# Scan mixer in a diffusion trunk: one exponential per head for both directions, convolution taps and gates in PSUM, heads in column halves

## The chip, the cores and the metric

The kernel runs on one core of a Trainium2 chip. The metric is the device time of one execution in microseconds (us); smaller is better. TensorE is written PE (its weight loads PEld), VectorE DVE, ScalarE ACT, GpSimd POOL, SyncE SP.

## What is computed

A trunk of four layers over 256 context tokens and 256 latent tokens of width 1024, in fp32. Layer 0 mixes tokens by differential attention, layer 1 by windowed attention, layer 2 by a scan in both directions, layer 3 again by differential attention; each mixer is followed by a gated FFN. The change is in layer 2's mixer, whose scan is this (32 heads in 4 groups, chunks of 128 tokens, both streams projected by one weight):

```python
xbc = silu(dwconv_centred(zxbcdt[...], conv_w, conv_b))       # 5 taps per channel
dt = softplus(zxbcdt[...] + dt_bias)                          # per direction and head
...
a_cs = cumsum(dt * A)                                         # within a chunk
seg = a_t[..., :, None] - a_t[..., None, :]
decay_in = exp(where(tril, seg, -inf))
cb = einsum('bclgn,bcsgn->bcgls', Cc, Bc)
y_diag = einsum('bcgls,bcghls,bcsghp->bclghp', cb, decay_in, xdt)
y_off = einsum('bclgn,bcghpn,bclgh->bclghp', Cc, prev, exp(a_cs))
...
y = (y_f + flip(y_b) + xs * d_skip) * silu(z)                 # then a norm and the output product
```

## The kernel before

All activations are kept feature-major, 128 features by 512 tokens (256 of context, 256 of latents). Weights come from HBM in fp32 by SP's queue; load_w (L255) splits each into a high and a low part, the high part by ACT (wh, L264), the low part by POOL (wl, L266), and lin (L283) makes each product of three matmuls, L291 to L293. All code is written straight-line; a scheduler sets each engine's order from the tiles' dependencies and the buffers that are free, and each engine then works through its list in that order. Names such as sc, sm, mm are tags: a tag has as many buffers as PSB or the tile's bufs say.

PSUM has eight banks: mm 2, ar 1, sc 2, sm 2, ad 1. In psum (L238) mm also takes the ar bank while no modulation rows are held, and the bank ad goes to the tag that EXTRA names for the mixer at work; for the scan mixer that is mm. So its products rotate over four banks, and sc has two.

ssd_mixer (L1287) goes through four groups of eight heads. A group has ten weight chunks: B, C, four of x, four of the gate z. chunk (L1304) is a product and conv_silu (L1076): ACT copies the product into a padded tile xpad (L1083), writes tap 0 with the bias into acc (L1089), DVE adds taps 1 to 4 one after another (L1097, in SBUF), ACT takes the tanh (L1100), DVE the last multiply (L1102). gate (L1310) halves the product by ACT (L1317), takes a tanh (L1318) and multiplies (L1319). In group 0 the two streams are projected one after the other, then ssd_dt (L1126) makes dt by a series on DVE (L1132 to L1146), the cumulative sums acs by small matmuls, and rows, the sums along the free dimension.

ssd_core (L1181) runs twice per group on four heads each. It transposes x to tokens, makes the chunk states (L1222 to L1236), and then for each head and each direction d: PE spreads a row of sums over all partitions (rb, L1247), POOL multiplies C·B by dt into cd (L1250), ACT makes four 128-wide steps Relu(acs - rb) into m (L1256), ACT takes exp(-m) (L1259), DVE multiplies m by cd (L1260). DVE then adds the two directions (L1262), and PE multiplies with the head's tokens into one half of the columns of yd (L1266), four matmuls of 128 columns. cd has two buffers (CDB), m three (DMB). After two heads DVE adds the skip term (L1271), and for each direction ACT takes er = exp(rb) (L1283), DVE multiplies it by the state product yo (L1284) and adds it to x (L1285). POOL also adds the squares for the group norm (L1340); finish (L1344) scales by it.

Of the kernel before, what the change touches and what calls it, by code (L numbers as in the profile page):

```python
# [180 lines left out]
class Trunk:  # L181
# [11 lines left out]
    EXTRA = ('sm', 'sc', 'mm')  # L193
    ENG_GATE = ENG_YO = 'vector'
    ENG_SSQ = 'gpsimd'
    ENG_CD = 'gpsimd'
    ENG_MADD = 'vector'
    ACTTAP = 0
# [157 lines left out]
    def ada_rows(self, i):  # L356
# [10 lines left out]
        self.acc = self.t([P, 6, 2, KD, 2], "acc")  # L367
# [261 lines left out]
    def ffn(self, i, u, streams, pool, gate, after, nxt):  # L629
# [53 lines left out]
        if nxt is not None:  # L683
            self.ada_rows(nxt)
# [391 lines left out]
    def conv_silu(self, ps, ci, dst, s, pool):  # L1076
# [9 lines left out]
        acc = self.t([P, 2, HALF], "cw", self.CW, pool=pool)[:, :ns]  # L1086
# [5 lines left out]
        if self.ACTTAP:  # L1092
            tm = self.t([P, 2, HALF], "cw", self.CW, pool=pool)[:, :ns]
            nc.scalar.activation(tm, xp[:, s0:s1, 4 : 4 + HALF], AF.Copy, scale=tap(4))
            nc.gpsimd.tensor_tensor(out=acc, in0=acc, in1=tm, op=AL.add)
        for j in range(1, 5 - self.ACTTAP):
# [29 lines left out]
    def ssd_dt(self, ps, pool):  # L1126
# [4 lines left out]
        v, e, q, p = w(), w(), w(), w()  # L1131
# [16 lines left out]
        self.dtt, at, self.acs, self.wst, self.dec = one("dtt"), one("at"), one("acs"), one("wst"), one("dec")  # L1148
# [15 lines left out]
        nc.scalar.activation(self.acs, acv, AF.Copy)  # L1164
        nc.scalar.activation(self.dec, totv, AF.Exp)
# [15 lines left out]
    def ssd_core(self, g, hf, bc, xf, sc, pool):  # L1181
# [58 lines left out]
        for j in range(2):  # L1240
            yd = self.psum("sc")
            for hh in (2 * j, 2 * j + 1):
                ms = []
                for d in range(2):
                    hd = 32 * d + h0 + hh
                    rb = self.psum("sc")
                    nc.tensor.matmul(rb, sel[d][:, hh, :], self.rows, start=True, stop=True)  # L1247
                    m = self.t([P, NT], "dm", self.DMB, pool=pool)
                    cd = self.t([P, NT], "cd", self.CDB, pool=pool)
                    getattr(nc, self.ENG_CD).tensor_tensor(  # L1250
                        out=cd.rearrange("p (c l) -> p c l", c=4), in0=cbm[d].rearrange("p (c l) -> p c l", c=4),
                        in1=self.dtt[:, :, hd : hd + 1].to_broadcast([P, 4, P]), op=AL.mult,
                    )
                    for c in range(4):
                        t = slice(c * P, (c + 1) * P)
                        nc.scalar.activation(  # L1256
                            m[:, t], rb[:, t], AF.Relu, scale=-1.0, bias=self.acs[:, c, hd : hd + 1]
                        )
                    nc.scalar.activation(m, m, AF.Exp, scale=-1.0)  # L1259
                    tt(out=m, in0=m, in1=cd, op=AL.mult)  # L1260
                    ms.append(m)
                getattr(nc, self.ENG_MADD).tensor_tensor(out=ms[0], in0=ms[0], in1=ms[1], op=AL.add)  # L1262
                r = 64 * (hh % 2)
                for c in range(4):
                    t = slice(c * P, (c + 1) * P)
                    nc.tensor.matmul(  # L1266
                        yd[r : r + 64, t], xtok[:, c, 64 * hh : 64 * hh + 64], ms[0][:, t], start=True, stop=True,
# [4 lines left out]
            for d in range(2):  # L1272
# [258 lines left out]
```

## Time and profile before

| | |
|---|---|
| median of three runs | 2726.39 us (2724.1 to 2736.12) |
| the profiled execution | 2728.86 us, its span 2726.7 us |
| PE busy | 2531.5 us (93%) |
| DVE busy | 1648.1 us (60%) |
| ACT busy | 1234.0 us (45%) |
| POOL busy | 1089.7 us (40%) |
| mean granted PE clock | 0.974 of full speed |

Shares are means over all stages. The scan mixer lies between about 1340 and 1890 us, its eight runs of ssd_core between 1425 and 1845. Busy time of an engine counts an instruction from its start to its end, waiting inside it included.

### The profile page before, as it was taken

The page shows a single profiled execution, that of the slowest core. Times are in us where ns is not written, and L with a number is a line of the kernel's source. Part 1 is how long each engine was busy: PE and PEld are TensorE (multiplying, and loading weights), DVE is VectorE, ACT ScalarE, POOL GpSimd, SP SyncE. Part 2 cuts the span into 40 slices and gives each one's busy share as a digit, 9 for nine tenths or more (in the row PEclk, how much of TensorE's full clock was granted, in tenths as well). Part 3 has the DMA queues.
Part 4 walks back from the last instruction along what each step waited for, and adds up shares of the span by engine and source line. Part 5 has one row for each costly group of instructions (what it writes and reads, how often), then busy time and mean ns, then how long its engine had stood idle before and what let it go on. Part 6 is the DMA issues. An engine that isn't in the chain of part 4 may idle for free.

```text
span 2726.7 us, 37430 instructions
## 1 busy us (share of the span) xinstructions
PE 2531.5 (93%) x13570; PEld 2089.7 (77%) x13570; DVE 1648.1 (60%) x3844; ACT 1234.0 (45%) x2514; POOL 1089.7 (40%) x525
## 2 busy tenths in 40 slices
PE   7899999999999999999988888889999998997998
PEld 4777688888776798888876666667988887876997
DVE  3776649931567649921689898866485116667112
ACT  5454553222557653222545565554432225555543
POOL 3322044444321054444243445442544443433784
PEclk9999999999999999999989899999999999999999
DMA  8333437742231147732221111123486323323452
GB/s 319 116 102 122 149 99 260 255 151 93 94 101 47 46 140 263 265 113 94 99 86 39 56 53 60 65 77 108 142 299 239 99 94 104 105 88 130 147 185 78
DMA packets 108040, 353.29 MB, mean 130 GB/s; under 512 B 14032, under 2 KB 24656, under 8 KB 105808
## 3 DMA queue, kind: packets, MB, share of 16 engines
q1 hardware_dynamic: 107280, 349.57, 38.1%
q8 instruction: 107, 1.75, 0.3%
q10 hardware_dynamic: 576, 1.34, 0.1%
q14 instruction: 77, 0.63, 0.1%
HBM read 329.36 MB, written 11.53 MB: 125 GB/s over the span
## 4 chain that ended last, share of the span: by engine, by line
PE 67%; DVE 14%; ACT 5%; issue 3%; DMA 2%; POOL 2%; DVEq 0%; ACTq 0%; SPq 0%; POOLq 0%
PE mm L291 6%; PE mm L292 6%; PE mm L293 6%; PE sc L291 5%; PE sc L293 5%; PE sc L292 5%; PE mm L302 4%; PE mm L303 4%; PE mm L301 4%; DVE dm L1260 2%; DVE cw L1097 2%; PE sc L303 1%; PE sc L301 1%; PE sc L302 1%; POOL wl L266 1%
## 5 line engine op out<-in xcount | busy, mean ns | idle before, releaser
L266 POOL TENSOR_TENSOR wl<-wr,wh 128x1024 fp32r<-128x1024 f32 x356 | 856.1, 2411 | 1354.9 <-ACT wh L264 1216.2
L264 ACT ACTIVATE wh<-wr 128x1024 fp32r<-128x1024 f32 x356 | 377.0, 1061 | 756.8 <-issue 277.1
L291 PE MATMUL mm<-uh,wh 128*128 128x512 f32 (+1 forms) x1136 | 406.5, 358 | 9.0 <-ACT uh L560 8.4
L293 PE MATMUL mm<-uh,wl 128*128 128x512 f32 (+1 forms) x1136 | 406.0, 357 | 0.0
L292 PE MATMUL mm<-ul,wh 128*128 128x512 f32 (+1 forms) x1136 | 405.4, 357 | 0.5 <-DVE sublng L861 0.4
L644 DVE TENSOR_TENSOR sc<-sc,sg 128x512 f32<-128x512 f32 (+1 forms) x100 | 57.5, 575 | 430.0 <-PE sc L293 423.2
L291 PE MATMUL sc<-uh,wh 128*128 128x512 f32 (+1 forms) x800 | 273.0, 341 | 0.7 <-DVE hid L647 0.7
L293 PE MATMUL sc<-uh,wl 128*128 128x512 f32 (+1 forms) x800 | 272.4, 341 | 0.0
L292 PE MATMUL sc<-ul,wh 128*128 128x512 f32 (+1 forms) x800 | 272.4, 340 | 0.0
L291 PEld LDWEIGHTS mm<-uh,wh 128*128 128x128 f32 x1136 | 219.6, 193 | 41.3 <-ACT uh L560 9.0
L292 PEld LDWEIGHTS mm<-ul,wh 128*128 128x128 f32 x1136 | 219.2, 193 | 30.2 <-issue 2.5
L293 PEld LDWEIGHTS mm<-uh,wl 128*128 128x128 f32 x1136 | 219.2, 193 | 27.8 <-issue 1.8
L303 PE MATMUL mm<-wl,hid 128*128 128x512 f32 x444 | 176.1, 397 | 0.0
L301 PE MATMUL mm<-wh,hid 128*128 128x512 f32 x444 | 176.1, 397 | 0.0
L302 PE MATMUL mm<-wh,hid 128*128 128x512 f32 x444 | 175.8, 396 | 0.0
L291 PEld LDWEIGHTS sc<-uh,wh 128*128 128x128 f32 x800 | 152.2, 190 | 17.7 <-DVE hid L647 0.9
L292 PEld LDWEIGHTS sc<-ul,wh 128*128 128x128 f32 x800 | 151.9, 190 | 16.8
L293 PEld LDWEIGHTS sc<-uh,wl 128*128 128x128 f32 x800 | 151.9, 190 | 16.9
L390 DVE SCALAR_TENSOR_TENSOR sq<-wa,sm 128x512 f32<-128x512 f32 x224 | 145.1, 677 | 0.1
L266 POOL TENSOR_TENSOR wl<-wa,wh 128x1024 fp32r<-128x1024 f32 x49 | 117.9, 2406 | 56.4 <-ACT wh L264 56.0
L1250 POOL TENSOR_TENSOR cd<-h,dtt 128x512 f32<-128x512 f32 x64 | 78.6, 1233 | 123.7 <-DVE dm L1260 117.6
L291 PE MATMUL ar<-uh,wh 128*128 128x256 f32 (+1 forms) x352 | 120.6, 343 | 0.0
(415 smaller groups left out, 5735.0 us busy)
## 6 DMA issues: line engine op xcount, KB each, us to landing
wr<-in_fin SPq DMA_DIRECT2D x154, 512.0 KB, 3.5
wa<-in_adat SPq DMA_DIRECT2D x144, 512.0 KB, 4.8
wr<-in_fout SPq DMA_DIRECT2D x77, 512.0 KB, 3.5
wr<-in_ssi SPq DMA_DIRECT2D x40, 512.0 KB, 3.5
wa<-in_adaw SPq DMA_DIRECT2D x36, 512.0 KB, 5.3
wr<-in_daqk SPq DMA_DIRECT2D x24, 512.0 KB, 3.7
wa<-in_fin SPq DMA_DIRECT2D x22, 512.0 KB, 3.5
wr<-in_sso SPq DMA_DIRECT2D x16, 512.0 KB, 3.5
```

The lines of the kernel that those rows point to most:

```text
L264: nc.scalar.activation(h, raw, AF.Copy)
L266: eng.tensor_tensor(out=l, in0=raw, in1=f32(h), op=AL.subtract)
L291: mm(out, wh, ah[ka][:, a:b], start=j == 0, stop=False)
L292: mm(out, wh, al[ka][:, a:b], start=False, stop=False)
L293: mm(out, wl, ah[ka][:, a:b], start=False, stop=j == len(todo) - 1)
L301: mm(out, ah[ka][:, tk], wt.h[:, kw, :], start=j == 0, stop=False)
L302: mm(out, al[ka][:, tk], wt.h[:, kw, :], start=False, stop=False)
L303: mm(out, ah[ka][:, tk], wt.l[:, kw, :], start=False, stop=j == len(todo) - 1)
L390: nc.vector.scalar_tensor_tensor(out=self.t([P, D], "sq", 2)[:, :512], in0=w[:, x, :], scalar=1.0, in1=self.arows[r, x], op0=AL.mult, op1= ...
L644: nc.vector.tensor_tensor(out=pu[:, :w], in0=pu[:, :w], in1=sg[:, :w], op=AL.mult)
L1097: nc.vector.scalar_tensor_tensor(out=acc, in0=xp[:, s0:s1, j : j + HALF], scalar=tap(j), in1=acc, op0=AL.mult, op1=AL.add)
L1250: getattr(nc, self.ENG_CD).tensor_tensor(out=cd.rearrange("p (c l) -> p c l", c=4), in0=cbm[d].rearrange("p (c l) -> p c l", c=4), in1=sel ...
```

## The change

In ssd_core the two directions of a head share one exponential. POOL multiplies C·B by dt for both directions (now L1245, into cd and m) and adds them (L1249): the two masked halves don't overlap but on the diagonal. PE spreads both rows into two PSUM banks. ACT writes rb[0] - acs into a tile f (L1257, four steps, with the negated sums nacs), DVE writes min(rb[1] - acs, f) into rb[1] (L1258, four steps), ACT takes one exponential in place in PSUM (L1262), DVE one multiply by cd (L1263). The tile f has one buffer, tag tf, which er uses too. The matmuls into yd come after both heads and alternate between the two column halves (L1269). er is no longer overwritten: DVE multiplies into yo in PSUM (L1287) and adds from there (L1288).

In conv_silu the sum of taps stays in the product's PSUM bank until the last multiply (L1087 to L1096); in gate the product is read from its bank and not halved, and the half goes into the multiply with y (L1335). ssd_dt runs after the latent stream's dt product, ahead of that stream's gates. EXTRA gives the bank ad to sc: three banks for sc, three for mm. The accumulators acc of the modulation's row sums come from the FFN's pool, and a pad tile is gone. Switches that were off (ACTTAP, ZB, ENG_GATE and others) are removed.

```diff
-    EXTRA = ('sm', 'sc', 'mm')
...
+    EXTRA = ('sm', 'sc', 'sc')
...
-        self.acc = self.t([P, 6, 2, KD, 2], "acc")
+        self.acc = self.t([P, 6, 2, KD, 2], "acc", pool=pool)
...
-        acc = self.t([P, 2, HALF], "cw", self.CW, pool=pool)[:, :ns]
+
+        acc = ps[:, : ns * HALF].rearrange("p (s t) -> p s t", s=ns)
...
         cbm = (sc["cbu"], sc["cbl"])
         for j in range(2):
-            yd = self.psum("sc")
+            ms = {}
             for hh in (2 * j, 2 * j + 1):
-                ms = []
+                hd = [32 * d + h0 + hh for d in range(2)]
+                m = ms[hh] = self.t([P, NT], "dm", self.DMB, pool=pool)
+                cd = self.t([P, NT], "cd", self.CDB, pool=pool)
+                eng = getattr(nc, self.ENG_CD)
+                for d, o in enumerate((cd, m)):
+                    eng.tensor_tensor(
+                        out=o.rearrange("p (c l) -> p c l", c=4), in0=cbm[d].rearrange("p (c l) -> p c l", c=4),
+                        in1=self.dtt[:, :, hd[d] : hd[d] + 1].to_broadcast([P, 4, P]), op=AL.mult,
+                    )
+                eng.tensor_tensor(out=cd, in0=cd, in1=m, op=AL.add)
+
+                rb = [self.psum("sc") for _ in range(2)]
                 for d in range(2):
...
-                    for c in range(4):
-                        t = slice(c * P, (c + 1) * P)
-                        nc.scalar.activation(
-                            m[:, t], rb[:, t], AF.Relu, scale=-1.0, bias=self.acs[:, c, hd : hd + 1]
-                        )
-                    nc.scalar.activation(m, m, AF.Exp, scale=-1.0)
-                    tt(out=m, in0=m, in1=cd, op=AL.mult)
-                    ms.append(m)
-                getattr(nc, self.ENG_MADD).tensor_tensor(out=ms[0], in0=ms[0], in1=ms[1], op=AL.add)
-                r = 64 * (hh % 2)
+                    nc.tensor.matmul(rb[d], sel[d][:, hh, :], self.rows, start=True, stop=True)
+                f = self.t([P, NT], "tf", 1, pool=pool)
                 for c in range(4):
                     t = slice(c * P, (c + 1) * P)
+                    nc.scalar.activation(f[:, t], rb[0][:, t], AF.Identity, bias=self.nacs[:, c, hd[0] : hd[0] + 1])
+                    stt(
+                        out=rb[1][:, t], in0=rb[1][:, t], scalar=self.acs[:, c, hd[1] : hd[1] + 1], in1=f[:, t],
+                        op0=AL.subtract, op1=AL.min,
+                    )
+                nc.scalar.activation(rb[1], rb[1], AF.Exp)
+                tt(out=m, in0=rb[1], in1=cd, op=AL.mult)
+            yd = self.psum("sc")
+            for c in range(4):
+                t = slice(c * P, (c + 1) * P)
+                for hh in (2 * j, 2 * j + 1):
+                    r = 64 * (hh % 2)
...
-                er = self.t([P, NT], "dm", self.DMB, pool=pool)
+                er = self.t([P, NT], "tf", 1, pool=pool)
...
-                    tt(out=er[:, t], in0=yo[:, t], in1=er[:, t], op=AL.mult)
-                    getattr(nc, self.ENG_YO).tensor_tensor(out=x[:, t], in0=x[:, t], in1=er[:, t], op=AL.add)
+                    tt(out=yo[:, t], in0=yo[:, t], in1=er[:, t], op=AL.mult)
+                    tt(out=x[:, t], in0=yo[:, t], in1=x[:, t], op=AL.add)
...
-            nc.scalar.activation(z[:, a:b], ps[:, :w], AF.Copy, scale=0.5)
             nc.scalar.activation(th[:, :w], ps[:, :w], AF.Tanh, scale=0.5)
             nc.vector.scalar_tensor_tensor(
-                out=z[:, a:b], in0=th[:, :w], scalar=1.0, in1=z[:, a:b], op0=AL.add, op1=AL.mult
+                out=z[:, a:b], in0=th[:, :w], scalar=1.0, in1=ps[:, :w], op0=AL.add, op1=AL.mult
             )
...
                     project_dt(wd, s)
+                    if s == "l":
+                        self.ssd_dt(pdt, pool)
                     for n in range(4):
                         gate(wz[n], zs[n], s)
                     for n in range(2):
                         chunk(ws[n], dst[n], ci[n], s)
-                self.ssd_dt(pdt, pool)
```

On DVE, in the middle of a run of ssd_core, before: dm is m, cd POOL's product, cw the convolution's sum and tanh, xpad its padded input, sm the state product.

```order
L1262 TENSOR_TENSOR dm_13675<-dm_13675,dm_13686 128x512
L1236 TENSOR_TENSOR h_12671<-sm_13668,h_12671 128x256
L1097 SCALAR_TENSOR_TENSOR cw_13912<-xpad_2552_12684,cwt_12672,cw_13912 128x512 x3
L1260 TENSOR_TENSOR dm_13702<-dm_13702,cd_13703 128x512
L1102 SCALAR_TENSOR_TENSOR bc_13837<-cw_13913,cw_13912 128x512
L1260 TENSOR_TENSOR dm_13713<-dm_13713,cd_13714 128x512
L1284 TENSOR_TENSOR dm_13734<-sm_13730,dm_13734 128x384
L1262 TENSOR_TENSOR dm_13702<-dm_13702,dm_13713 128x512
```

Now, in the same place: sc is the head's second bank of spread rows, tf the tile f, mm the bank that holds a chunk's sum of taps.

```order
L1258 SCALAR_TENSOR_TENSOR sc_13723<-sc_13723,acs_12986,tf_13726 128x128
L1335 SCALAR_TENSOR_TENSOR o_86<-o_86 128x512
L1258 SCALAR_TENSOR_TENSOR sc_13723<-sc_13723,acs_12986,tf_13726 128x128
L1091 SCALAR_TENSOR_TENSOR mm_13885<-xpad_2552_12686,cwt_12671,mm_13885 128x512
L1258 SCALAR_TENSOR_TENSOR sc_13723<-sc_13723,acs_12986,tf_13726 128x128
L1091 SCALAR_TENSOR_TENSOR mm_13925<-xpad_2551_12683,cwt_12671,mm_13925 128x512
L1258 SCALAR_TENSOR_TENSOR sc_13723<-sc_13723,acs_12986,tf_13726 128x128
L1096 SCALAR_TENSOR_TENSOR o_86<-cw_13911,mm_13885 128x512
L1091 SCALAR_TENSOR_TENSOR mm_13925<-xpad_2551_12683,cwt_12671,mm_13925 128x512 x2
L1263 TENSOR_TENSOR dm_13717<-sc_13723,cd_13718 128x512
```

A head's three operations on two SBUF tiles have become four narrow ones on PSUM, between which taps stand, and one multiply from PSUM.

On POOL, in the first run of ssd_core, before: h is the spilled C·B, dtt the dt, wl a weight's low part.

```order
L1250 TENSOR_TENSOR cd_13460<-h_12671,dtt_13179 128x512
L1250 TENSOR_TENSOR cd_13471<-h_12671,dtt_13179 128x512
L1250 TENSOR_TENSOR cd_13487<-h_12671,dtt_13179 128x512
L266 TENSOR_TENSOR wl_14379<-wr_14377,wh_14378 128x1024
L1250 TENSOR_TENSOR cd_13498<-h_12671,dtt_13179 128x512
```

Now, from the third head on:

```order
L1245 TENSOR_TENSOR dm_13436<-h_12670,dtt_12985 128x512
L1245 TENSOR_TENSOR cd_13437<-h_12670,dtt_12985 128x512
L1249 TENSOR_TENSOR cd_13437<-cd_13437,dm_13436 128x512
L263 TENSOR_TENSOR wl_14206<-wr_14204,wh_14205 128x1024
L1245 TENSOR_TENSOR cd_13457<-h_12670,dtt_12985 128x512
L1245 TENSOR_TENSOR dm_13456<-h_12670,dtt_12985 128x512
L1245 TENSOR_TENSOR dm_13644<-h_12670,dtt_12985 128x512
L1249 TENSOR_TENSOR cd_13457<-cd_13457,dm_13456 128x512
L263 TENSOR_TENSOR wl_14246<-wr_14244,wh_14245 128x1024
```

Each head has three operations where it had two, and a weight split stands behind an add that waits for both products.

On PE, the product of a head's m with its tokens, before: one head at a time, between matmuls of a chunk (ar) and transposes (sm).

```order
L293 MATMUL ar_13968<-uh_84,wl_13882 128x512
L291 MATMUL ar_13968<-uh_84,wh_13881 128x512
L292 MATMUL ar_13968<-ul_85,wh_13881 128x512
L1207 MATMUL sm_13622<-cst_base_67,o_86 128x128 x4
L293 MATMUL ar_13968<-uh_84,wl_13882 128x512
L1266 MATMUL sc_13456<-dm_13486,h_12671 64x128 x4
L291 MATMUL ar_13968<-uh_84,wh_13881 128x512
```

Now the two heads of a pair alternate; the pair's first matmul stands 18 rows further up.

```order
L289 MATMUL ar_13845<-ul_85,wh_13550 128x512
L290 MATMUL ar_13845<-uh_84,wl_13551 128x512
L1269 MATMUL ad_13476<-dm_13456,h_12670 64x128
L1269 MATMUL ad_13476<-dm_13436,h_12670 64x128
L1269 MATMUL ad_13476<-dm_13456,h_12670 64x128
L1269 MATMUL ad_13476<-dm_13436,h_12670 64x128
L1269 MATMUL ad_13476<-dm_13456,h_12670 64x128
L1269 MATMUL ad_13476<-dm_13436,h_12670 64x128
L1269 MATMUL ad_13476<-dm_13456,h_12670 64x128
L1253 MATMUL sc_13650<-rows_13037,sel_13608 128x512
```

Both heads' m must be there before the last seven; no matmul of the chunk stands between them any more.

## Rows read from the trace of the kernel before

**Rows 1.** The page: DVE's busy tenths in 40 slices, and the last chain.

```profile
DVE  3776649931567649921689898866485116667112
...
PE 67%; DVE 14%; ACT 5%; issue 3%; DMA 2%; POOL 2%; DVEq 0%; ACTq 0%; SPq 0%; POOLq 0%
```

**Rows 2.** By stretch: length; PE, PEld, DVE, ACT, POOL busy; clock; DMA share; GB/s.

```profile
500.00:600.00 100.00, 100.00 (x438) 81.99 (x437) 64.78 (x185) 25.64 (x30) 45.54 (x19) 1.00 0.62 201
800.00:900.00 100.00, 92.39 (x509) 64.19 (x507) 75.49 (x237) 73.42 (x214) 14.27 (x6) 1.00 0.16 47
1340.00:1390.00 50.00, 46.97 (x370) 45.73 (x371) 36.87 (x59) 29.31 (x61) 24.49 (x15) 1.00 0.44 141
1390.00:1425.00 35.00, 28.22 (x148) 22.82 (x147) 27.09 (x35) 12.03 (x20) 8.47 (x4) 0.80 0.16 53
1425.00:1845.00 420.00, 348.70 (x1611) 266.04 (x1610) 359.06 (x531) 232.35 (x546) 181.70 (x110) 0.93 0.18 60
```

**Rows 3.** Groups by line, 1425 to 1845: count; busy us, mean ns; idle before.

```profile
L1097 DVE SCALAR_TENSOR_TENSOR cw<-xpad,cwt,cw 128x512 f32<-128x512 f32 x82 | 81.2, 991 | 1.5 <-ACT cw L1089 0.6
L1250 POOL TENSOR_TENSOR cd<-h,dtt 128x512 f32<-128x512 f32 x64 | 78.6, 1233 | 123.7 <-DVE dm L1260 117.6 <-DVE h L1199 5.4 <-PE mm L292 0.7
L1260 DVE TENSOR_TENSOR dm<-dm,cd 128x512 f32<-128x512 f32 x64 | 70.4, 1103 | 33.2 <-ACT dm L1259 30.4 <-POOL cd L1250 2.7
L1262 DVE TENSOR_TENSOR dm<-dm,dm 128x512 f32<-128x512 f32 x32 | 39.9, 1246 | 0.1
L1222 DVE TENSOR_TENSOR v<-h,wst 128x256 f32<-128x256 f32 x48 | 28.3, 620 | 0.8 <-PE sm L1227 0.4 <-ACT h L1208 0.3
L1285 DVE TENSOR_TENSOR o<-o,dm 128x384 f32<-128x384 f32 (+2 forms) x47 | 24.3, 552 | 0.0
L1284 DVE TENSOR_TENSOR dm<-sm,dm 128x384 f32<-128x384 f32 (+2 forms) x47 | 19.5, 415 | 1.6 <-ACT dm L1283 1.6
L1232 DVE TENSOR_TENSOR h<-h,dec 128x256 f32<-128x256 f32 x32 | 18.0, 562 | 2.5 <-ACT h L1230 2.5
L1102 DVE SCALAR_TENSOR_TENSOR o<-cw,cw 128x512 f32<-128x512 f32 x15 | 13.1, 872 | 2.1 <-ACT cw L1100 2.1
```

**Rows 4.** Groups by line and shape, DVE, 1370 to 1900; columns as before.

```profile
L1284 DVE TENSOR_TENSOR dm<-sm,dm 128x384 f32<-128x384 f32 x16 | 8.8, 547 | 0.0
L1284 DVE TENSOR_TENSOR dm<-sm,dm 128x128 f32<-128x128 f32 x16 | 4.5, 284 | 1.6 <-ACT dm L1283 1.6
```

**Rows 5.** Single lines, whole span: count; duration ns least/median/most; first and last start; shapes.

```profile
L1260 DVE TENSOR_TENSOR dm<-dm,cd x64: 672/691/2872, 1428.5 to 1837.8; 128x512 f32<-128x512 f32 x64
L1271 DVE SCALAR_TENSOR_TENSOR o<-o,sng,sc x16: 734/746/748, 1449.0 to 1843.6; 128x512 f32<-128x512 f32 x16
L516 DVE SCALAR_TENSOR_TENSOR sc<-sc,rs_y,h x27: 742/749/752, 332.3 to 2721.7; 128x512 f32<-128x512 f32 x27
L1250 POOL TENSOR_TENSOR cd<-h,dtt x64: 1046/1112/2037, 1426.6 to 1828.6; 128x512 f32<-128x512 f32 x64
L1340 POOL TENSOR_TENSOR sq<-sq x12: 1267/1292/3026, 1479.6 to 1847.5; 128x512 f32<-128x512 f32 x12
```

**Rows 6.** Waits, 1425 to 1845: who <- for whom: us in total, times, longest.

```profile
POOL cd L1250 <- DVE dm L1260: 117.6, 47, 10.3
...
PE sc L1266 <- DVE dm L1262: 36.4, 26, 6.9
```

**Rows 7.** Instructions of PE in order of time: start us, us, line.

```profile
830.08 1.08 PE L1055 MATMUL sm<-swt,swv 128*64 128x256 f32 x8
...
1561.10 1.09 PE L1266 MATMUL sc<-dm,h 128*64 128x128 f32 x8 [0.27 <-DVE dm L1262]
```

**Rows 8.** Instructions of DVE in order of time: two chunks' first taps and last steps.

```profile
1570.21 3.90 DVE L1097 SCALAR_TENSOR_TENSOR cw<-xpad,cwt,cw 128x512 f32<-128x512 f32 x4
...
1576.24 0.68 DVE L1102 SCALAR_TENSOR_TENSOR bc<-cw,cw 128x512 f32<-128x512 f32 x1
...
1581.62 0.74 DVE L1097 SCALAR_TENSOR_TENSOR cw<-xpad,cwt,cw 128x512 f32<-128x512 f32 x1
...
1601.28 1.58 DVE L1102 SCALAR_TENSOR_TENSOR bc<-cw,cw 128x512 f32<-128x512 f32 x1
```

More of the change, by code (lines that the diff above doesn't have):

```diff
@@ L192 @@
     HEAD = 4
-    EXTRA = ('sm', 'sc', 'mm')
-    ENG_GATE = ENG_YO = 'vector'
+    EXTRA = ('sm', 'sc', 'sc')
     ENG_SSQ = 'gpsimd'
     ENG_CD = 'gpsimd'
-    ENG_MADD = 'vector'
-    ACTTAP = 0
     BC = 4
@@ L352, in ada_finish, with ada_rows @@
                 tt(out=mv, in0=pj, in1=gain, op=AL.mult)
-    def ada_rows(self, i):
+    def ada_rows(self, i, pool):
         nc = self.nc
@@ L683, in ffn @@
         if nxt is not None:
-            self.ada_rows(nxt)
+            self.ada_rows(nxt, pool)
         for p in range(0, n):
@@ L1091, in conv_silu @@
         )
[L1092 to L1096, printed above, removed]
+        for j in range(1, 5):
             nc.vector.scalar_tensor_tensor(
@@ L1130, in ssd_dt @@
         w = lambda: self.t([P, NT], "cw", self.CW, pool=pool)[:64]
-        v, e, q, p = w(), w(), w(), w()
+        v, e, p = w(), w(), w()
+        q = ps[:64]
         ts(out=v, in0=ps[:64], scalar1=self.dtp[:, 0:1], scalar2=None, op0=AL.add)
@@ L1147, in ssd_dt @@
         one = lambda n: self.t([P, 4, 64], n, pool=pool)
-        self.dtt, at, self.acs, self.wst, self.dec = one("dtt"), one("at"), one("acs"), one("wst"), one("dec")
+        self.dtt, self.acs, self.nacs, self.wst, self.dec = (one(n) for n in ("dtt", "acs", "nacs", "wst", "dec"))
+        at = self.t([P, HALF], "v", 4, pool=pool).rearrange("p (c h) -> p c h", c=4)
         for src, dst in ((v, self.dtt), (e, at)):
@@ L1164, in ssd_dt @@
         nc.scalar.activation(self.acs, acv, AF.Copy)
+        nc.scalar.activation(self.nacs, acv, AF.Copy, scale=-1.0)
         nc.scalar.activation(self.dec, totv, AF.Exp)
@@ L1240, in ssd_core @@
         for j in range(2):
-            yd = self.psum("sc")
+            ms = {}
             for hh in (2 * j, 2 * j + 1):
-                ms = []
-                for d in range(2):
[L1245 to L1252, printed above, removed]
-                    )
-                    for c in range(4):
-                        t = slice(c * P, (c + 1) * P)
-                        nc.scalar.activation(
-                            m[:, t], rb[:, t], AF.Relu, scale=-1.0, bias=self.acs[:, c, hd : hd + 1]
-                        )
-                    nc.scalar.activation(m, m, AF.Exp, scale=-1.0)
-                    tt(out=m, in0=m, in1=cd, op=AL.mult)
-                    ms.append(m)
-                getattr(nc, self.ENG_MADD).tensor_tensor(out=ms[0], in0=ms[0], in1=ms[1], op=AL.add)
-                r = 64 * (hh % 2)
@@ L1266, in ssd_core @@
+                nc.scalar.activation(rb[1], rb[1], AF.Exp)
[5 more added lines that the diff above has]
+                    r = 64 * (hh % 2)
                     nc.tensor.matmul(
-                        yd[r : r + 64, t], xtok[:, c, 64 * hh : 64 * hh + 64], ms[0][:, t], start=True, stop=True,
+                        yd[r : r + 64, t], xtok[:, c, 64 * hh : 64 * hh + 64], ms[hh][:, t], start=True, stop=True,
@@ L1331, in ssd_mixer @@
             zs = self.o[4 * ((g + 1) % 2) : 4 * ((g + 1) % 2) + 4]
-            for n in range(self.ZB):
-                zs[n] = self.t([P, NT], "zs", self.ZB, pool=pool)
             def gated(n):
-                getattr(nc, self.ENG_GATE).tensor_tensor(out=xg[n], in0=xg[n], in1=zs[n], op=AL.mult)
+                nc.vector.scalar_tensor_tensor(
+                    out=xg[n], in0=xg[n], scalar=0.5, in1=zs[n], op0=AL.mult, op1=AL.mult
+                )
                 d = 2 * (n > 0)
@@ L1479, in run @@
             self.prenorm(m[0], m[1], t)
-        self.t([P, 8], "pad")
         for n, (i, mix, ff) in enumerate(self.layers):
```

## The prediction, made before the changed kernel ran

> **What bounds the kernel now.** I read the slices first, then the busy table by stage, then the groups of the one stage that stands out, then single rows. Outside the scan mixer there is little to win: in the FFN the matmuls fill the engine, 100.00 of 100 us at clock 1.00 [rows 2]. In the slices DVE is at 9 tenths in one long block only, the scan mixer, and DVE holds 14% of the chain that ended last [rows 1]. By stage, from 1425 to 1845 us (the eight runs of ssd_core, 420 us) DVE is busy 359.06 us, PE 348.70 at a mean clock of 0.93, ACT 232.35, POOL 181.70 [rows 2]. DVE is the bound there: it idles 61 us, PE 71 us, and PE's largest waits are for L1262, the add that ends a head on DVE (36.4 us in 26 waits) [rows 6].
>
> What fills DVE is not arithmetic. L1260 multiplies two SBUF tiles: its fastest is 672 ns, its median 691, its longest 2872 [rows 5], its mean in this stage 1103 [rows 3]. The spread has the size of a POOL instruction: the two POOL forms here take 1112 and 1292 ns [rows 5]. The operations with one operand in PSUM show no spread: L1271 lies between 734 and 748 ns in 16 executions, L516, which reads and writes PSUM, between 742 and 752 in 27 [rows 5]. So DVE's operations on two SBUF tensors wait while POOL works, those with a PSUM operand do not.
>
> **The change part by part, core stage.** All sums are in DVE time of 1425 to 1845.
> The heads. Before, each of 32 heads costs two L1260 and one L1262: 70.4 + 39.9 = 110.3 us [rows 3]. After, it costs four 128-wide subtract-and-min operations and one 512-wide multiply, all with a PSUM operand. The multiply is 0.69 (the 691 of an undisturbed one). For the 128-wide one no row stands; L1284 goes from 547 ns at 384 columns to 284 at 128 [rows 4], 1.03 ns a column, so L516's 749 at 512 columns gives about 0.35 at 128. Sum: 32 x 0.69 + 128 x 0.35 = 66.9 us, **43.4 saved**. Undisturbed, the old form would cost 96 x 0.69 = 66.2 us: the arithmetic is no cheaper, all of the gain is waiting that disappears.
> The taps. 82 at 991 ns [rows 3] become PSUM in and out, 749 (L516's form): **19.8 saved**. The last step of the convolution: 15 at 872 [rows 3] become 0.69, **2.7 saved**; I don't count the rest of them and the gates.
> The off-diagonal add (L1285, 24.3) takes its other operand from PSUM and then costs what L1284 costs at the same sizes, 19.5 [rows 3]: **4.8 saved**.
> Against this, what stays on two SBUF tensors meets a busier POOL. L1222 and L1232 take 28.3 and 18.0 us [rows 3]; by an undisturbed 0.41 us for 256 columns (between L1284's 284 and 547) their 80 would take 32.8, so 13.5 us is waiting. POOL's share rises: 64 cd products at 1.112 and 32 new adds at 1.292 (L1340's form) make 112.5 where L1250 had 78.6, so 215.6 us of some 350 instead of 181.7 of 420, 62% for 43%. That scales 13.5 to 19.4: **6 lost**. DVE in sum: 43.4 + 19.8 + 2.7 + 4.8 - 6 = 64.7 us less.
>
> The other engines. ACT loses four of eight 128-wide steps and one of two exponentials per head, and has 188 us of idle time to begin with; it only gets lighter. PE: 348.70 busy at 0.93 would be 324 at full clock, less what the column halves give: eight matmul records of 256 columns on alternating halves take 1.08 us (L1055), eight of 128 columns, a head on one half, 1.09 (L1266) [rows 7], so alternating is twice as fast and up to 14 us of PE can go. At 420 - 65 = 355 us PE would be 87 to 91% busy, as in the attention mixer (92.39 of 100 [rows 2]): no bound yet, with little room left. I take nothing for it; that is the reserve under the larger gain below.
> POOL: at the start of a group a head waited for one cd product; now it waits for two products and an add. That is 1.112 + 1.292 = 2.4 us at three group starts, **7 lost** if nothing covers it; elsewhere its queue runs ahead, as today, where POOL waits 117.6 us for DVE to free cd [rows 6]. What queues behind a cd that waits is wl, the weight split that PE needs two chunks later.
>
> **Front of the mixer.** ssd_dt's chain moves from behind the two streams to ahead of the latent stream's gates. From 1390 to 1425 PE is busy 28.22 us at clock 0.80, 22.6 us' worth: 12.4 us are lost there, the bound of this gain; zero is the other. DVE has room, busy 64 of 85 us from 1340 [rows 2]. The chain then lies beside six half-width products: I take **10**, near the upper end, since nothing else holds PE there.
> The accumulators' new pool, the dropped pad, nacs (one copy) and the gate's halving moved into a multiply cost or give nothing I can price: all lie on DVE or ACT beside a full PE.
>
> Sum: -65 + 7 - 10 = -68 us. The profiled execution took 2728.86, 2.5 above the median; from it 2661, from the median of 2726.39 **2658 us**.
>
> [...]
>
> **The rivals.**
> 1. Half comes back as waiting. The products and the scan share more serial pieces: one tf tile serves all heads and both exponentials of the off-diagonal part, and a head's two selector banks are two of three. DVE's freed time then turns into idle time. For it: the engines run in a fixed order, and DVE already waits 61 us. Against: the two chains of four ACT steps per head become one. Half of 65, with the other terms: -33 + 7 - 10, **2690 us**.
> 2. More than forecast. If PE closes its idle time: 71 us of gaps and 348.70 x 0.07 = 24 us of slow clock, with 12 in front, -107: **2619 us**. It needs DVE to stop being late everywhere.
> 3. The change doesn't do what it says: operations with a PSUM operand wait for POOL as well when they also read SBUF, as the taps will. The heads then save nothing. +7 - 10: **2723 us**. Against: 43 undisturbed executions in two rows [rows 5].
> 4. Slower: the chunk's PSUM bank. Today four banks serve the products, each free after one copy; now there are three, held until the last step of the convolution. From first tap to last step is 1570.21 to 1576.92 in one chunk, 1581.62 to 1602.86 in another [rows 8]. With about 8 us of product and ACT before it a bank is held 15 to 29 us; six such and four gates of some 9 make 126 to 210 us per group on three banks, 42 to 70 us, under the 105 us that a group takes now. It decides from 46 us a chunk; at 50 a group takes 112 us, four of them 28 us more: **2754 us**. Against: the taps get shorter.
>
> **How the numbers follow.** Forecast 0.52, rival 1 0.21, rival 2 0.14, rival 3 0.07, rival 4 0.06. The range goes from rival 2 to a little beyond rival 1, 2618 to 2702, and leaves 3 and 4 out. About 0.5% (13.6 us) is what a measurement of this kernel tells from no change: forecast, 1 and 2 are faster by more (0.87), 3 is the same (0.07), 4 slower (0.06).
>
> **What would show it.** Right: the multiply at 0.69 us with hardly a spread, taps near 0.75, the small steps near 0.35; DVE some 295 us busy in a core stage of about 355; the clock there above 0.95; POOL near 216. Wrong: long waits of PE for a bank of mm or ar that DVE releases (rival 4); ACT waiting for the tf tile (rival 1); a multiply with a mean above 1 us (rival 3); DVE waiting for cd at many heads, which would make POOL's third operation dearer than 7 us.

## The result, and the profile after

| | before | after |
|---|---|---|
| median | 2725.24 us (2723.34 to 2736.12, 4 runs) | 2682.69 us (2681.79 to 2685.07, 4 runs) |
| ratio | 1 | 0.9837, 95% interval 0.981 to 0.9864 |
| profiled run / its span | 2728.86 / 2726.7 us | 2682.53 / 2680.7 us |

The change makes the kernel 44 us faster (37 to 52 by the interval); the forecast was 68. Its parts are best read in three places. First the single operations, over the whole span (count; duration ns least/median/most; first and last start; shapes). After the change L1263 is a head's multiply, L1258 its 128-wide step, L1091 a tap:

```profile
L1263 DVE TENSOR_TENSOR dm<-sc,cd x22: 676/691/693, 1420.5 to 1773.2; 128x512 f32<-128x512 f32 x22
L1258 DVE SCALAR_TENSOR_TENSOR sc<-sc,acs,tf x88: 345/354/364, 1415.6 to 1771.1; 128x128 f32<-128x128 f32 x88
L1091 DVE SCALAR_TENSOR_TENSOR mm<-xpad,cwt,mm x68: 476/748/757, 1360.4 to 1702.4; 128x512 f32<-128x512 f32 x60, 128x256 f32<-128x256 f32 x8
```

There is no spread left: the multiply's longest is 693 ns, where L1260's was 2872 [rows 5]. Second the groups of the core stage of after, 1415 to 1778 (count; busy us, mean ns; idle before), against [rows 3]:

```profile
L1091 DVE SCALAR_TENSOR_TENSOR mm<-xpad,cwt,mm 128x512 f32<-128x512 f32 x56 | 41.9, 748 | 1.3 <-ACT mm L1087 1.3
L1219 DVE TENSOR_TENSOR v<-h,wst 128x256 f32<-128x256 f32 x48 | 41.3, 911 | 2.2 <-ACT h L1205 1.9 <-PE sm L1224 0.3
...
L1258 DVE SCALAR_TENSOR_TENSOR sc<-sc,acs,tf 128x128 f32<-128x128 f32 x88 | 31.1, 354 | 2.6 <-ACT tf L1257 0.6
...
L1229 DVE TENSOR_TENSOR h<-h,dec 128x256 f32<-128x256 f32 x32 | 21.1, 660 | 2.1 <-ACT h L1227 2.1
L1091 DVE SCALAR_TENSOR_TENSOR ar<-xpad,cwt,ar 128x512 f32<-128x512 f32 x28 | 20.9, 747 | 0.0
...
L1263 DVE TENSOR_TENSOR dm<-sc,cd 128x512 f32<-128x512 f32 x22 | 15.1, 686 | 11.2 <-ACT sc L1262 10.4 <-POOL cd L1249 0.6
...
L1258 DVE SCALAR_TENSOR_TENSOR ad<-ad,acs,tf 128x128 f32<-128x128 f32 x40 | 14.1, 352 | 0.5
...
L1263 DVE TENSOR_TENSOR dm<-ad,cd 128x512 f32<-128x512 f32 x10 | 6.9, 686 | 2.7 <-ACT ad L1262 2.5
```

The heads cost 15.1 + 6.9 + 31.1 + 14.1 = 67.2 us of DVE, where they had cost 110.3. But L1219 (L1222 before) grew from 28.3 to 41.3.

Third the stretches (length; PE, PEld, DVE, ACT, POOL busy; clock; DMA share; GB/s). The whole mixer of before, up to a point 827 us ahead of the end (in the second half of the out-projection, whose last matmul starts 12 us later), and from its last off-diagonal add (1845.6) to that point:

```profile
1340.00:1900.00 560.00, 477.90 (x2378) 378.75 (x2379) 454.81 (x702) 297.62 (x676) 225.79 (x133) 0.94 0.22 72
1846.00:1900.00 54.00, 53.01 (x251) 43.33 (x250) 30.82 (x78) 23.40 (x50) 11.13 (x5) 1.00 0.32 111
```

The same of after: the mixer, its core, and from the last off-diagonal add (1777.4) to the same point of the program:

```profile
1340.00:1850.00 510.00, 458.74 (x2368) 362.32 (x2367) 390.57 (x766) 234.90 (x491) 253.32 (x164) 0.95 0.24 78
1415.00:1778.00 363.00, 326.96 (x1605) 247.98 (x1604) 300.53 (x600) 171.45 (x373) 204.99 (x140) 0.95 0.21 67
1778.00:1850.00 72.00, 66.33 (x305) 53.34 (x304) 38.19 (x77) 28.82 (x54) 21.06 (x9) 1.00 0.32 110
```

The last off-diagonal add comes 68 us earlier, the very number of the forecast. From there to the common point in the out-projection it is 54 us before and 72 after: 18 us are given back there, with PE busy 66 of 72 us at clock 1.00. The first output of the out-projection, which stands behind the last products of the mixer in PE's queue, comes at 1766.9 where it came at 1817.3 (lines under run 11): 50 us earlier, as much as the whole mixer gained.

```profile
L1408 ACT ACTIVATE o<-mm x5: 598/600/614, 1766.9 to 1806.1; 128x512 f32<-128x512 f32 x5
```

Some 4 us more go in the attention mixer that follows; this is one stretch of it in the kernel before, then the one that answers in the changed kernel:

```profile
2300.00:2400.00 100.00, 87.20 (x558) 76.60 (x557) 64.83 (x137) 51.88 (x110) 38.71 (x23) 0.95 0.34 108
```

```profile
2250.00:2350.00 100.00, 84.70 (x532) 74.71 (x531) 63.69 (x134) 49.97 (x107) 36.10 (x22) 0.93 0.33 104
```

PE's granted clock there is 0.93 where it was 0.95, with nothing of the change in that stage; why is not shown.

Seen from PE the mixer became 50 us shorter: 19 us less busy, 31 us less idle. Two of PE's waits in the mixer (us in total, times, longest), for the state update's two steps on DVE, before and then after:

```profile
PE sm L1227 <- DVE v L1222: 10.1, 8, 3.0
PE sm L1227 <- DVE h L1236: 2.2, 1, 2.2
```

```profile
PE sm L1224 <- DVE h L1233: 14.2, 6, 3.8
PE sm L1224 <- DVE v L1219: 7.2, 10, 2.6
```

These are PE's largest waits now: with the heads no longer late, the chain of states is.

### The profile page after: what moved, and what is told of

Its sections match the earlier page's. It is cut to its first block, busy times and chain, and to the rows that moved or that the text cites. A ratio compares the mean times of both kernels' runs of the same rounds, so it can differ in the third digit from the quotient of the medians.

```text
span 2680.7 us, 37406 instructions
## 1 busy us (share of the span) xinstructions
PE 2511.5 (94%) x13570; PEld 2073.0 (77%) x13570; DVE 1584.2 (59%) x3908; ACT 1173.8 (44%) x2335; POOL 1118.8 (42%) x557
## 5 line engine op out<-in xcount | busy, mean ns | idle before, releaser
L263 POOL TENSOR_TENSOR wl<-wr,wh 128x1024 fp32r<-128x1024 f32 x356 | 853.5, 2404 | 1362.3 <-ACT wh L261 1231.7
L288 PE MATMUL mm<-uh,wh 128*128 128x512 f32 (+1 forms) x1184 | 426.2, 360 | 13.2 <-ACT uh L557 6.9
L289 PE MATMUL mm<-ul,wh 128*128 128x512 f32 (+1 forms) x1184 | 424.3, 358 | 0.6 <-DVE sublng L858 0.5
L290 PE MATMUL mm<-uh,wl 128*128 128x512 f32 (+1 forms) x1184 | 424.5, 359 | 0.0
L288 PEld LDWEIGHTS mm<-uh,wh 128*128 128x128 f32 x1184 | 228.8, 193 | 47.1 <-ACT uh L557 7.1
L289 PEld LDWEIGHTS mm<-ul,wh 128*128 128x128 f32 x1184 | 228.2, 193 | 30.6 <-issue 1.9
L290 PEld LDWEIGHTS mm<-uh,wl 128*128 128x128 f32 x1184 | 228.2, 193 | 29.4 <-issue 1.8
L298 PE MATMUL mm<-wh,hid 128*128 128x512 f32 x454 | 180.0, 396 | 0.0
L299 PE MATMUL mm<-wh,hid 128*128 128x512 f32 x454 | 179.7, 396 | 0.0
L263 POOL TENSOR_TENSOR wl<-wa,wh 128x1024 fp32r<-128x1024 f32 x49 | 117.8, 2405 | 59.8 <-ACT wh L261 57.1
L288 PE MATMUL ar<-uh,wh 128*128 128x256 f32 (+1 forms) x400 | 135.2, 338 | 5.3 <-DVE o L1096 2.2
L289 PE MATMUL ar<-ul,wh 128*128 128x256 f32 (+1 forms) x400 | 135.5, 339 | 0.0
```

Of the source, the lines that this page charges most:

```text
L263: eng.tensor_tensor(out=l, in0=raw, in1=f32(h), op=AL.subtract)
L288: mm(out, wh, ah[ka][:, a:b], start=j == 0, stop=False)
L289: mm(out, wh, al[ka][:, a:b], start=False, stop=False)
L290: mm(out, wl, ah[ka][:, a:b], start=False, stop=j == len(todo) - 1)
L298: mm(out, ah[ka][:, tk], wt.h[:, kw, :], start=j == 0, stop=False)
L299: mm(out, al[ka][:, tk], wt.h[:, kw, :], start=False, stop=False)
```

## The experiments

Theory A: PE's queue sets the mixer's end; what DVE saves counts only as far as it closes idle time of PE. Theory B, the prediction's: DVE's queue sets it. Times are differences from runs of the kernel before on the same chip, ratio minus one times some 2728 us; the whole change stands at -44.

**1. Taps and gates back in SBUF.**
```diff
-        acc = ps[:, : ns * HALF].rearrange("p (s t) -> p s t", s=ns)
+        acc = self.t([P, 2, HALF], "cw", self.CW, pool=pool)[:, :ns]
...
+            nc.scalar.activation(z[:, a:b], ps[:, :w], AF.Copy, scale=0.5)
...
```


> The changed kernel with one part undone: the scan's taps and gates are built in SBUF again, as in the kernel before, while the heads keep the new form. The theory (VectorE's two-SBUF operations wait for GpSimd, and TensorE now fills most of the mixer): the 68 taps of the mixer's main part go from 0.75 back to about 0.95 to 1.0 us with a wide spread, so VectorE works about 20 us longer, but it has idle time by now, so the whole is only 6 to 14 us longer than the changed kernel (2689 to 2697). Rival, VectorE's sum still sets the time: the full 20 us (2703). Rival, the taps' place does not matter: 0.


Measured: ratio 0.9951 (0.9936 to 0.9966), -13 us, so 31 us of the gain are gone, more than either theory gave and nearer to B's price than to A's. The expectation counted 68 taps, those that the changed kernel makes in the bank mm; this stage has 85. Its taps, and its mixer:

```profile
L1091 DVE SCALAR_TENSOR_TENSOR cw<-xpad,cwt,cw 128x512 f32<-128x512 f32 x85 | 95.2, 1120 | 0.8 <-ACT cw L1087 0.6
```

```profile
1340.00:1888.00 548.00, 472.75 (x2386) 369.62 (x2385) 445.60 (x772) 245.87 (x517) 267.49 (x164) 0.93 0.22 72
```

The taps' mean is 1120 ns, not the 991 of before [rows 3]: beside the new heads, with POOL busy 267 of 548 us in the mixer where it was 226 of 560, a tap on two SBUF tensors waits longer. DVE has 55 us more than in the changed kernel (445.60 against 390.57), and the mixer is 38 us longer.

**2. Taps and gates in PSUM alone, in the kernel before** (the reverse of the same edit).


> The kernel before with one part of the change alone: the taps and gates are in PSUM, the heads stay as they were. The theory: the taps take 0.75 us without a spread instead of 0.99, about 20 us of VectorE's work, in a stage that VectorE bounds: 12 to 20 us shorter than the kernel before (2705 to 2713). Rival, TensorE bounds the stage anyway: under 6 us. With the other run, the two parts of the change should add up to the 43 us of the whole.


Measured: 0.9934 (0.9918 to 0.9951), -18 us. Its mixer:

```profile
1340.00:1874.00 534.00, 471.76 (x2365) 371.15 (x2364) 401.00 (x699) 287.04 (x650) 219.43 (x132) 0.94 0.23 75
```

DVE lost 54 us (454.81 to 401.00), the mixer 26, the time 18. The parts alone give -13 and -18, the whole -44; the three intervals leave some 10 us of doubt on the 13 us between. DVE's sum can't explain that: with the taps done, the heads take only 10 us more from DVE (401.00 to 390.57) and 26 us from the time. PE's two sums go down by 13 busy and 11 idle on that step. POOL's work is that of before here, and most of what stays on two SBUF tensors waits less than before, not longer (means of 1103 and 620 ns before [rows 3]; only L1232 goes the other way, 18.0 to 23.0 us in sum):

```profile
L1260 DVE TENSOR_TENSOR dm<-dm,cd 128x512 f32<-128x512 f32 x64 | 57.1, 894 | 25.5 <-ACT dm L1259 21.8 <-POOL cd L1250 2.8 <-POOL wl L266 0.3
L1222 DVE TENSOR_TENSOR v<-h,wst 128x256 f32<-128x256 f32 x48 | 24.0, 539 | 2.4 <-ACT h L1208 2.4
```

**3. ssd_dt in its old place.** 
```diff
-                    if s == "l":
-                        self.ssd_dt(pdt, pool)
...
+                self.ssd_dt(pdt, pool)
                 for n in range(2, 4):
                     chunk(nw(n), dst[n], ci[n], "b")
```


> The changed kernel with the decay sums and softplus (ssd_dt) issued in their old place. The prediction put 10 us on their earlier place, within 0 and 12.4. If that term is real, this run is about 10 us longer (2693). If TensorE's total work in the mixer sets the time, the matmuls that follow fill the wait, and it is 0 to 4 us longer (2683 to 2687).


Measured: 0.9831 (0.9816 to 0.9845), -46 us: the new place is worth nothing. In the profiles the first core's first add then starts 6 us later (1444.5 for 1438.3) and the last 2.6 us earlier (1774.8 for 1777.4).

**4. The output matmuls one half of the columns after the other.**
```diff
-            for c in range(4):
-                t = slice(c * P, (c + 1) * P)
-                for hh in (2 * j, 2 * j + 1):
+            for hh in (2 * j, 2 * j + 1):
+                for c in range(4):
```


> The changed kernel with its output matmuls of a head pair issued all for one half of TensorE's columns and then all for the other, instead of in turn. The theory (TensorE's work in the mixer is fixed and sets the time): these matmuls go back from 26 us in the main part to about 41 us, and nearly all of the 15 us shows in the time (2694 to 2698). Rival, VectorE sets the time in the main part: TensorE hides it, 0 to 3 us.


Measured: 0.9858 (0.9843 to 0.9873), -39 us, 6 us of the gain gone by the middles of two intervals that overlap (9 by the spans, 2689.8 for 2680.7; 7 against run 3, whose four times all lie below this run's). First the changed kernel's groups of these matmuls in the mixer, then this one's:

```profile
L1269 PE MATMUL sc<-dm,h 128*64 128x128 f32 x176 | 17.8, 290 | 0.0
L1269 PE MATMUL ad<-dm,h 128*64 128x128 f32 x80 | 8.2, 290 | 0.0
```

```profile
L1269 PE MATMUL sc<-dm,h 128*64 128x128 f32 x176 | 25.8, 293 | 0.8 <-DVE dm L1263 0.7
L1269 PE MATMUL ad<-dm,h 128*64 128x128 f32 x80 | 12.0, 291 | 0.7 <-DVE dm L1263 0.7
```

26.0 us against 37.8: alternating takes 11.8 us off PE, and half or more of it shows in the time. The prediction took nothing for it.

**5. The exponential into SBUF**, so that the multiply has two SBUF operands.
```diff
-                nc.scalar.activation(rb[1], rb[1], AF.Exp)
-                tt(out=m, in0=rb[1], in1=cd, op=AL.mult)
+                nc.scalar.activation(m, rb[1], AF.Exp)
+                tt(out=m, in0=m, in1=cd, op=AL.mult)
```


> The changed kernel with one operand moved: the exponential of a head is written into the SBUF tile that the multiply then reads, instead of over its PSUM bank, so the multiply of the 32 heads in the mixer's main part has two SBUF operands instead of one. The theory (only operations with two SBUF operands wait for GpSimd): the multiply's mean goes from 0.69 to about 1.0 to 1.3 us with a wide spread, 10 to 20 us more of VectorE, and the time rises by 5 to 15 us (2688 to 2698). Rival, the multiply gained because it takes half the operations (one exponential for both directions) and the operand's place is nothing: its mean stays at 0.69 and the time at 2683.


Measured: 0.9852 (0.9831 to 0.9874), -40 us; the price in time can't be told from zero. The operation itself answers, as a group of the core stage and over the whole span:

```profile
L1263 DVE TENSOR_TENSOR dm<-dm,cd 128x512 f32<-128x512 f32 x32 | 35.5, 1110 | 8.4 <-ACT dm L1262 7.5
```

```profile
L1263 DVE TENSOR_TENSOR dm<-dm,cd x32: 677/692/2477, 1417.0 to 1773.4; 128x512 f32<-128x512 f32 x32
```

The median is the same 0.69 us, the mean 1110 instead of 686 ns: the place of one operand decides, as the prediction had it. 13.5 us more of DVE's time cost 4 us by the middles of the two intervals.

**6. Two tf tiles** (one cw buffer less, for the room).
```diff
-    CW = 4
+    CW = 3
...
-                f = self.t([P, NT], "tf", 1, pool=pool)
+                f = self.t([P, NT], "tf", 2, pool=pool)
...
-                er = self.t([P, NT], "tf", 1, pool=pool)
+                er = self.t([P, NT], "tf", 2, pool=pool)
```


> The changed kernel with two buffers of the tile tf instead of one (and three of the pool cw instead of four, for the room). The prediction's first rival said that the single tf tile gives part of the gain back as waiting; after the change ScalarE shows 25 us of idle time released by the last readers of tf. If that decides, this run is 7 to 15 us faster (2668 to 2676). If the waits lie beside TensorE's work, it stays within 3 us (2680 to 2686).


Measured: 0.984 (0.9815 to 0.9864), -44 us: nothing. The last off-diagonal add starts 8 us earlier (1769.4 for 1777.4), and the time does not follow. The tf tile (rival 1) is not what took the gain, as far as the missing cw buffer hides nothing.

**7. Four mm banks, two sc.**
```diff
-    EXTRA = ('sm', 'sc', 'sc')
+    EXTRA = ('sm', 'sc', 'mm')
```


> The changed kernel with its PSUM banks split another way: four of the pool mm and two of sc, where the change has three and three (with two heads' banks, the two sums of a head and the pair's output then share two). The prediction's fourth case said that three mm banks, held to a run's last tap, stop TensorE; the trace of the changed kernel shows 8.4 us of TensorE waiting for those banks. If they set the time, this run is 4 to 8 us faster (2675 to 2679). If the third sc bank is worth more, it is slower, by up to 20 us (2683 to 2703).


Measured: 0.9842 (0.9825 to 0.9859), -43 us: nothing, though the last off-diagonal add starts 6 us later (1783.7). PE's wait for the gate's mm bank goes from 4.2 to 1.4 us, while PE then waits 5.7 us for the multiply's tile. Rival 4's banks are not it either.

**8. Two of the four added taps left out.**
```diff
-        for j in range(1, 5):
+        for j in range(1, 3):
```


> The changed kernel without the last two of the scan's four added taps, in every stage: that leaves 52 of 104 operations of 0.75 us on VectorE out of the mixer, 39 us, and touches no other engine's work. Theory A (TensorE's fixed work sets the time by now): at most 12 us faster (2671 or more). Theory B (VectorE's queue still sets the time of the main part): about 30 us or more faster (2645 to 2653).


Measured: 0.9802 (0.9783 to 0.9821), -54 us, 9.5 faster than the change by the middles; the intervals just overlap, but all four times lie below the change's four. Its mixer:

```profile
1340.00:1842.00 502.00, 455.88 (x2388) 362.07 (x2387) 363.91 (x716) 237.60 (x497) 255.98 (x165) 0.96 0.24 81
```

DVE has 27 us less than in the changed kernel, not the 39 of the expectation, and the mixer is 8 us shorter; PE's idle time is 46 instead of 51 us. As theory A says; B's 30 us don't come.

**9. 64 matmuls of the out-projection's first half left out.**
```diff
             mm(out, al[ka][:, tk], wt.h[:, kw, :], start=False, ...)
-            mm(out, ah[ka][:, tk], wt.l[:, kw, :], start=False, stop=j == len(todo) - 1)
+            if low:
+                mm(out, ah[ka][:, tk], wt.l[:, kw, :], start=False, stop=j == len(todo) - 1)
...
-                self.lin_tokens(ps, bs, yh, yl, t)
+                self.lin_tokens(ps, bs, yh, yl, t, False)
```


> The changed kernel without the third of the three matmuls (the one with the weights' low part) in the first half of the out-projection: 128 matmuls of 0.23 us and their weight loads, 29 us of TensorE, nothing of another engine. Most of these stand in the stretch behind the heads. Theory A (the out-projection is TensorE's work that used to fill the gaps and now stands behind the heads): nearly the whole 29 us off the time (2654 to 2660). Theory B (VectorE sets the time): under 12 us.


The expectation counted the matmuls double: there is one such mixer, so 64 x 0.23 = 14.6 us were left out. Measured: 0.9823 (0.9799 to 0.9846), -48 us, 4 faster than the change (6 by the spans), with intervals that overlap. By the middles that is a quarter to two fifths of the work taken away, too little for theory A in its plain form; the intervals reach from nothing to almost the whole. From the last add to the common point in the out-projection:

```profile
1777.00:1844.00 67.00, 58.20 (x242) 45.33 (x241) 36.38 (x77) 25.41 (x51) 17.68 (x8) 0.90 0.32 117
```

It is 5 us shorter than in the changed kernel (67 for 72), with 8 us less work: PE ran at clock 0.90 instead of 1.00, and idles 9 us instead of 6. But in the stretch just before, 1730 to 1777, the clock was 1.00 here and 0.93 in the changed kernel, and over the mixer 0.94 and 0.95: the slow stretch stands in another place. That fewer matmuls made the clock slower is not shown.

**10. The accumulators' pool and the pad alone, in the kernel before.**
```diff
-        self.acc = self.t([P, 6, 2, KD, 2], "acc")
+        self.acc = self.t([P, 6, 2, KD, 2], "acc", pool=pool)
...
-        self.t([P, 8], "pad")
```


> The kernel before with the smallest part of the change alone: the row sums' accumulators in the FFN's pool and no padding tile; nothing of the mixer. The prediction put it at nothing: within 3 us of the kernel before.


Measured: 1.0006 (0.9994 to 1.0018), +2 us: nothing, as forecast.

**11 and 12. DVE operations left out of one run of heads, in the kernel before**; 11 in the last run (g 3), 12 in the fourth (g 1).
```diff
+                if (g, hf) != (3, 1):
                     getattr(nc, self.ENG_MADD).tensor_tensor(out=ms[0], in0=ms[0], in1=ms[1], op=AL.add)
...
+                    if (g, hf) != (3, 1):
                         tt(out=er[:, t], in0=yo[:, t], in1=er[:, t], op=AL.mult)
                         getattr(nc, self.ENG_YO).tensor_tensor(out=x[:, t], in0=x[:, t], in1=er[:, t], op=AL.add)
```


> The kernel before, with part of VectorE's work of the last of the mixer's eight runs of heads left out: the sums of the two directions and the off-diagonal steps' multiply and add, 16 operations, about 10.5 us of VectorE by the means of the rows before (1.25, 0.40 and 0.51 us); no engine else loses work. Theory of the lag: in this last run TensorE already works ahead in the out-projection (120 of its matmuls stand there), so that what VectorE saves here is mostly covered: 0 to 4 us faster (2725 to 2729 where the kernel before has 2729). Rival, every us of VectorE's queue counts alike: 8 to 10.5 us faster.

> The same 16 operations (10.5 us of VectorE) left out of the kernel before, but in the fourth of the eight runs of heads, where TensorE has no out-projection to fill its gaps with. Theory of the lag: most of it counts, 7 to 10.5 us faster, clearly more than where they are left out of the last run. Rival, TensorE bounds the whole mixer: under 4 us in both places.


Measured: in the last run 1.002 (1.001 to 1.003), 5 us slower, which no theory forecast and no row explains; in the fourth 0.9993 (0.9982 to 1.0004), -2 us. Nothing is gained in either place, as in the rival for which PE bounds the whole; the lag theory, which gave the fourth run 7 us or more, misses. The off-diagonal add in the kernel before and in 12, and the skip term (L1271, here L1272) in 11 (first and last start):

```profile
L1285 DVE TENSOR_TENSOR o<-o,dm x48: 276/415/2612, 1449.8 to 1845.6; 128x384 f32<-128x384 f32 x16, 128x128 f32<-128x128 f32 x16, 128x256 f32<-128x256 f32 x16
```

```profile
L1287 DVE TENSOR_TENSOR o<-o,dm x42: 278/418/2617, 1453.7 to 1829.5; 128x384 f32<-128x384 f32 x14, 128x128 f32<-128x128 f32 x14, 128x256 f32<-128x256 f32 x14
```

```profile
L1272 DVE SCALAR_TENSOR_TENSOR o<-o,sng,sc x16: 733/748/749, 1446.8 to 1822.9; 128x512 f32<-128x512 f32 x16
```

The outputs of the out-projection's first half (PSUM to SBUF; first and last start), in the kernel before, then in 11, then in 12:

```profile
L1406 ACT ACTIVATE o<-mm x4: 580/592/615, 1817.3 to 1859.9; 128x512 f32<-128x512 f32 x4
...
L1406 ACT ACTIVATE o<-ad x2: 573/586/598, 1856.6 to 1865.5; 128x512 f32<-128x512 f32 x2
```

```profile
L1408 ACT ACTIVATE o<-mm x4: 579/596/657, 1817.6 to 1863.6; 128x512 f32<-128x512 f32 x4
```

```profile
L1408 ACT ACTIVATE o<-mm x4: 581/590/605, 1816.7 to 1864.5; 128x512 f32<-128x512 f32 x4
```

In 12 the last off-diagonal add is 16 us earlier than before (1829.5 for 1845.6), in 11 the last skip term 21 us earlier (1822.9 for 1843.6 [rows 5]). The first half of the out-projection starts within 1 us of 1817 and ends within 2 of 1865 in all three, and PE waits under 3 us in all for its inputs. So DVE's end does not set the out-projection's time in the kernel before; what stands ahead of it in PE's queue does. Waits and mixer of 12:

```profile
PE sc L1267 <- DVE dm L1263: 22.4, 19, 4.2
PE sm L1227 <- DVE v L1222: 16.0, 7, 7.3
```

```profile
1340.00:1900.00 560.00, 480.65 (x2385) 380.38 (x2384) 448.50 (x687) 298.69 (x676) 229.50 (x134) 0.94 0.21 73
```

PE's wait for the heads' add fell by 14 us, from 36.4 [rows 6] to 22.4. But its wait for v rose from 10.1 to 16.0, smaller ones rose too, and busy time rose by 3: the sum stays at 560.

## Why the prediction was right, and where its size was off

**DVE's terms held, but one.** The multiply is 0.69 us, the 128-wide step 0.35, the taps 0.75, all without a spread; the heads cost 67.2 us (forecast 66.9). The off-diagonal add now costs 0.417 us a piece, like L1284 before (0.415 [rows 3]):

```profile
L1288 DVE TENSOR_TENSOR o<-sm,o 128x384 f32<-128x384 f32 (+2 forms) x48 | 19.0, 417 | 0.2
```

Run 5 shows the reason by itself, one operand's place. The trace of the changed kernel shows the wait: L1219, on two SBUF tensors, takes from 410 to 2584 ns, a spread of 2174, and POOL's weight split there takes 2437 on average. 22 of L1219's 48 start while POOL is idle and take 410 to 426 ns; 26 start while a POOL instruction runs, and all but one of these take 684 ns or more and end 280 to 286 ns after that instruction's end. The operations with an operand in PSUM show none of this: of the 84 taps of 128x512 in the core, 42 start while a POOL instruction runs and take 740 to 757 ns, the other 42 take 740 to 762. A tap's median is 748 ns in PSUM and 746 in SBUF (run 1), 2 ns apart.

The term that was mis-sized is the "+6" for what stays on two SBUF tensors. L1219 and L1229 went from 28.3 + 18.0 to 41.3 + 21.1 us: 16 us, with POOL busy 205 of 363 us. That is 56%, less than the 62 of the forecast, so that scaling the old waiting by POOL's share was too kind. Of their 80 operations 37 take 500 ns or more, and each ends within 0.3 us of a POOL instruction's end: 27 of one of the heads' own (20 L1245, 7 L1249), 8 of a weight split (L263), 2 of the squares (L1341). DVE was busy 300.5 us in a core of 363 (forecast 295 of 355, of 362 with its own 7 us at group starts). That the last add came 68 us earlier, the very sum, is partly luck: 10 us too little in this term stand against the 7 that did not come.

**The step that failed** is the first, "DVE is the bound there", and with it the sum that put the core's end on the path. DVE had the larger busy share, but much of that was waiting. In the kernel before its end can move by 16 to 21 us with nothing behind it moving (runs 11 and 12), and in the changed kernel by 6 to 8 either way (runs 6 and 7). PE's queue sets the mixer's end, by its work and by its waits, and as most of these are for DVE in the middle of the runs, DVE counts in part: in the kernel before PE used its waits to run about 120 matmuls of the out-projection ahead of the last add, in the changed kernel about 70. The forecast counted PE's 71 us of gaps as room; beside PE's own work they were the only place the gain could come from. From 1340 on 31 us of idle time closed (82 to 51): the heads' wait of 36.4 us [rows 6] is gone (0.0 us before L1269), and other waits grew by 5, that for the state's h from 2.2 to 14.2. By the mixers of run 8 (DVE -27, mixer -8), run 2 (-54, -26) and run 1 (+55, +38) a microsecond of DVE was worth 0.3 to 0.7 of one: not a whole, and no fixed share.

**PE's reserve** was not nothing. Alternating halves take 12 us off PE (run 4), by the middles 6 to 9 of them off the time; the prediction had seen "up to 14" and left it out.

**POOL at group starts, +7**: DVE waits 0.6 us in all for the new add's cd, so about nothing. **Front, -10**: the heads do begin 10 us earlier, but run 3 shows that it is worth nothing: from 1340 to 1415 PE is busy 69.7 us there and 65.4 in the changed kernel, so the other order fills the same gap with work that is then done. **Memory**: nothing, right (run 10).

**The rivals.** Rival 1 has nearly the measured time (2690), not the mechanism: the single tf tile (run 6) and the banks cost nothing; what came back stands behind the core, on PE. Rival 2 asked for all of PE's idle time, and 31 of 82 us closed. Rival 3 is out (run 5). Rival 4's waits exist, at 8.4 us for all product banks (4.2 of them for a gate), and run 7 finds them free.

**Open**: why 10.5 us saved in the fourth run of heads give nothing at all. Its rows show the wait moving from the heads to the state update's v, and no run here separates the order of PE's instructions from the waits themselves. Why run 11 is 5 us slower stays open too, as does what the heads' new form is worth without the rest of the change: run 1 has everything but taps and gates, and no run takes alone the tile of ssd_dt that the change also keeps in PSUM.

## What to carry to other kernels

Where two engines are busy almost alike (here 85 and 83% of a stage), price an edit on the queue that starts the next stage (here PE's: its busy time plus its idle time by releaser), and cap the gain at the idle time that the edited engine causes there and the work it takes from that queue; a sum over the busiest engine's instructions gave the right core and the wrong end. Here the operations whose second operand went to PSUM stopped waiting for GpSimd (a tap's mean went from 991 to 748 ns; the multiply's is 686, and 1110 with that operand back in SBUF, run 5). Where the same edit gave GpSimd more work, those left on two SBUF tensors waited longer (L1219 from 620 to 911 ns), and moving the taps was worth more beside the new heads than without them; where GpSimd's work stayed the same (run 2), they waited less in sum (L1260, L1262 and L1222 busy 138.6 us before and 117.7 there, against 5 us more of L1232).

## What the hardware showed that was not expected

The two halves of the change are worth 13 and 18 us alone and 44 together. The same tap in SBUF takes 991 ns on average in the kernel before [rows 3] and 1120 beside the new heads (run 1), at a median of 746 there: the wait for POOL goes by what POOL does beside the operation (busy 226 of 560 us in the mixer of before, 267 of 548 in run 1). And the heads' output matmuls, 256 records of 128 columns, cost PE 26.0 us with the two column halves in turn and 37.8 one half after the other (run 4).
